# A two-layer diffusion step on one core: states and weights requested a step earlier, one gating result kept in SBUF, weight sums split in place

## The chip, the cores and the metric

The kernel runs on 1 core of one Trainium2 chip. The metric is device time in microseconds (us): the time that one launch takes on the core. Beside the times there is one profiled execution, whose trace records the instructions of each engine: PE (matmuls), DVE, ACT and POOL (elementwise work), and SP, whose queue issues the transfers.

## What is computed

A context of 128 tokens and 2048 latent tokens (2176 rows of 1024 numbers, float32) pass two layers, each with an RMS norm with scale and shift, an input projection, a mixer, an output projection and a gated residual. Layer 0, the one that the change touches, cut to what matters:

```python
q, k, v, ga, lr_f, lr_b, u, vs, gb = split_cols(h @ w_in_even, EVEN_SPLITS)
o_f, s_f = gla_scan(q, k, v, log_decay(lr_f, 0), s0_f)             # forward over the tokens
o_r, s_b = gla_scan(flip(q), flip(k), flip(v), flip(...), s0_b)    # backward
o_a = rmsnorm(o_f + flip(o_r), gla_norm_g) * silu(ga)              # branch A, 512 wide
sp  = einsum('hij,bnjhd->bnihd', w_s, rmsnorm(vs)) + b_s           # chunks of 128 tokens
o_b = u * sp * silu(gb)                                            # branch B, 512 wide
x   = x + gate * (concatenate([o_a, o_b]) @ w_out[0])
```

In `gla_scan` a state S of 64 x 128 for each head goes from one chunk of tokens to the next: `S = exp(b_last) * S + k'^T v`. Layer 1 has a pooling branch and a convolution branch; its input projection uses sums and differences of blocks of its weight matrix.

## The kernel before

A float32 product is made of three matmuls: every operand is kept as a rounded part *hi* (written by ACT) and the rest *lo* (DVE, or POOL for every third), both 128 x 512 for most tiles. `split` (L220) does that.

Layer 0 runs in four blocks of tokens (`block1`, L774; starts at about 0, 224, 415 and 612 us of the trace). A block makes its normed input `ring_hh`/`ring_hl` from `ring_xk` (`make_h`, L400), multiplies it with 20 groups of weight columns (`pg_g` is the PSUM tile of these products, two buffers), and has elementwise work evict each product. Weights come in through `load_w` (L229): raw from HBM and split in the first block that uses them, stored as hi and lo (`dr_w8h`, `dr_w8l`, for instance), and loaded from there in the later blocks (L235). Beside that, for every tile of 128 tokens, `gla_tile` computes the attention and the tile's contribution to the states: decays `Z` and `dec`, the contribution `ub` of the backward scan with its decay in a last column (L626, L627, L671), stored by L673 to `dr_ub`; the forward state `Sf` is stored by L664 to `dr_sf`.

Three pieces of work are put into this order a step at a time, one step after so many column groups (`tick`, L156; `side`, L183). A step ends at a `yield`.

- `prep_x` (L435) makes the next block's input: loads, squares summed on POOL, the norm, and then eight multiplications `make_t` on DVE (L391, 128 x 512). It begins after the first of the four gate groups.
- `weight_sums` (L743) makes 12 sets of sums for layer 1. A set loads two raw tiles of 128 x 1024 (L748), runs four POOL instructions (L760 to L768), stores one result to `dr_s` (L761), and splits three others (`part`): *hi* into a tile `px` (L753, ACT), *lo* over the sum itself (L755, DVE), and both stored to `dr_hl` (L757). The tag `px` has two buffers and is also used for the squares (L310). Two steps run at every third tick from the second block on; five steps are a set.
- The output projection of layer 0 (from about 869 us) runs over five blocks `BLKO`, the last tokens first, since the backward state goes from the last tile to the first. `finish_o` (L940) takes for each tile the state `Sb` from `states` (L922): two loads (L920, from `dr_sf` and `dr_ub`), then four DVE instructions (L934) that add the state of the tile after it, times its decay. Branch B's results lie in `dr_ob` (stored by L882, loaded back by `ob_part`). The first block `BLKO[0]` (tokens 1664 to 2176) is the last block of `block1`, and part of its work is done there.

A scheduler sets each engine's order when the kernel is built; an engine runs its instructions strictly in that order. All transfers are issued by SP from a single queue, also in order: where the next one waits for its data or its buffer, those behind it wait too. From about 1116 us on, layer 1 runs (four blocks of 544 tokens) to the end of the span.

## Time and profile before

| | us |
|---|---|
| median of 3 runs (lowest to highest) | 1888.07 (1882.71 to 1893.24) |
| the profiled execution | 1888.73 |
| its span in the trace | 1886.6 |
| PE busy | 1748.2 |
| DVE busy | 1196.5 |
| ACT busy | 845.5 |
| POOL busy | 741.6 |

The span is what the trace records from the first to the last instruction; the profiled execution takes 2.1 us more. In the views, `out<-in` names the tiles that an instruction writes and reads, and x4 is a count. PEclk is the clock that TensorE was granted, as a share of full speed; its two levels are 1.2 and 2.4 GHz. "Idle before" is the time that an engine sat idle ahead of an instruction, with the instruction or transfer that ended it; for a transfer, `a<-b` says that b was copied to a.

### The profile page before, as it was taken

The page shows a single profiled execution, that of the slowest core. Times are in us where ns is not written, and L with a number is a line of the kernel's source. Part 1 is how long each engine was busy: PE and PEld are TensorE (multiplying, and loading weights), DVE is VectorE, ACT ScalarE, POOL GpSimd, SP SyncE. Part 2 cuts the span into 40 slices and gives each one's busy share as a digit, 9 for nine tenths or more (in the row PEclk, how much of TensorE's full clock was granted, in tenths as well). Part 3 has the DMA queues.
Part 4 walks back from the last instruction along what each step waited for, and adds up shares of the span by engine and source line. Part 5 has one row for each costly group of instructions (what it writes and reads, how often), then busy time and mean ns, then how long its engine had stood idle before and what let it go on. Part 6 is the DMA issues. An engine that isn't in the chain of part 4 may idle for free. (4 is left out here: it accounts for less than half of the span.)

```text
span 1886.6 us, 39851 instructions
## 1 busy us (share of the span) xinstructions
PE 1748.2 (93%) x15115; PEld 1602.1 (85%) x15115; DVE 1196.5 (63%) x2270; ACT 845.5 (45%) x1795; POOL 741.6 (39%) x796
## 2 busy tenths in 40 slices
PE   5999899989999998999898999989999999999996
PEld 4877778768777897997687899989999999999996
DVE  5557852780679428656867775785758375837653
ACT  4544543451446326524534554554545354524431
POOL 0432543430453223335555562364335333532322
PEclk9999899999999998999898999999999999999998
DMA  9767787775766464476776478777977697659753
GB/s 327 270 227 252 283 301 251 250 252 209 279 224 227 147 242 149 148 231 180 235 243 213 140 264 263 248 254 260 320 241 227 208 326 241 217 189 329 233 185 130
DMA packets 232606, 444.15 MB, mean 235 GB/s; under 512 B 26208, under 2 KB 72032, under 8 KB 232416
## 3 DMA queue, kind: packets, MB, share of 16 engines
q1 hardware_dynamic: 232416, 441.62, 69.7%
q8 instruction: 119, 1.95, 0.4%
q14 instruction: 71, 0.58, 0.1%
HBM read 344.64 MB, written 96.88 MB: 234 GB/s over the span
## 5 line engine op out<-in xcount | busy, mean ns | idle before, releaser
L252 PE MATMUL pg_g<-t_t,wh_hi 128*128 128x272 f32 (+1 forms) x1920 | 371.0, 291 | 5.9 <-DVE tmp_ev L1328 3.0
L252 PEld LDWEIGHTS pg_g<-t_t,wh_hi 128*128 128x128 f32 x1920 | 302.1, 189 | 7.4 <-DVE tmp_ev L1328 3.6
L252 PE MATMUL pg_g<-t_t,wh_lo 128*128 128x280 f32 (+1 forms) x960 | 273.2, 290 | 2.0 <-DVE wh_lo L222 1.7
L252 PE MATMUL pg_g<-ring_hh,wp_hi 128*128 128x512 f32 (+2 forms) x632 | 234.8, 372 | 11.3 <-DVE tmp_ev L875 10.2
L252 PE MATMUL pg_g<-ring_hh,wp_lo 128*128 128x512 f32 (+2 forms) x632 | 230.4, 365 | 2.2 <-POOL wp_lo L222 1.9
L252 PE MATMUL pg_g<-ring_hl,wp_hi 128*128 128x512 f32 (+2 forms) x632 | 230.3, 364 | 0.0
L221 ACT ACTIVATE wh_hi<-wh_raw 128x512 fp32r<-128x512 f32 x208 | 130.6, 629 | 198.3 <-PE pg_g L252 137.7
L252 PEld LDWEIGHTS pg_g<-t_t,wh_lo 128*128 128x128 f32 x960 | 179.8, 189 | 2.8 <-DVE wh_lo L222 2.1
L252 PE MATMUL pg_g<-wp_hi,ring_hh 128*128 128x256 f32 (+1 forms) x528 | 161.0, 306 | 11.8 <-DMA wp_hi<-dr_w8h 3.3
L311 POOL TENSOR_TENSOR tmp_acc<-tmp_acc,tmp_px 128x512 f32<-128x512 f32 (+5 forms) x83 | 112.4, 1354 | 135.8 <-ACT tmp_px L310 132.2
L222 DVE TENSOR_TENSOR wh_lo<-wh_raw,wh_hi 128x512 fp32r<-128x512 f32 x156 | 125.8, 808 | 53.5 <-ACT wh_hi L221 44.6
L252 PE MATMUL pg_g<-wp_hi,ring_hl 128*128 128x256 f32 (+1 forms) x528 | 156.4, 298 | 3.4 <-DVE ring_hl L407 3.2
L252 PE MATMUL pg_g<-wp_lo,ring_hh 128*128 128x256 f32 (+1 forms) x528 | 156.6, 297 | 0.5 <-DMA wp_lo<-dr_w6l 0.5
L252 PE MATMUL px_x<-t_t,wh_hi 128*128 128x272 f32 (+1 forms) x768 | 151.3, 291 | 0.3 <-DVE tmp_ev L1277 0.3
L252 PEld LDWEIGHTS pg_g<-ring_hh,wp_hi 128*128 128x128 f32 x632 | 120.8, 191 | 31.6 <-DVE tmp_ev L875 10.7
L252 PE MATMUL pg_g<-o_oh,wh_hi 128*128 128x272 f32 (+2 forms) x448 | 130.4, 293 | 8.5 <-ACT o_oh L221 5.3
L252 PEld LDWEIGHTS pg_g<-ring_hh,wp_lo 128*128 128x128 f32 x632 | 121.0, 191 | 19.2 <-POOL wp_lo L222 2.1
L252 PEld LDWEIGHTS pg_g<-ring_hl,wp_hi 128*128 128x128 f32 x632 | 121.0, 191 | 14.8 <-issue 1.1
L252 PE MATMUL pg_g<-o_ol,wh_hi 128*128 128x272 f32 (+2 forms) x448 | 131.7, 295 | 1.3 <-DVE o_ol L222 1.3
L252 PE MATMUL pg_g<-o_oh,wh_lo 128*128 128x272 f32 (+2 forms) x448 | 131.3, 294 | 0.0
L566 POOL TENSOR_TENSOR gl_Z<-gl_Z 128x128 f32<-128x128 f32 x170 | 82.3, 504 | 124.6 <-DVE gl_Z L566 84.9
L550 ACT ACTIVATE gl_L<-gl_Z 128x256 f32<-128x256 f32 x204 | 83.2, 419 | 97.3 <-DVE gl_Z L566 75.5
(298 smaller groups left out, 4403.4 us busy)
## 6 DMA issues: line engine op xcount, KB each, us to landing
wh_raw<-in_w_dram SPq DMA_DIRECT2D x144, 256.0 KB, 3.6
wh_hi<-dr_hl SPq DMA_DIRECT2D x144, 256.0 KB, 3.5
wh_lo<-dr_hl SPq DMA_DIRECT2D x144, 256.0 KB, 3.9
wp_raw<-in_w_ada_dram SPq DMA_DIRECT2D x32, 512.0 KB, 5.1
wp_raw<-in_w_dram SPq DMA_DIRECT2D x24, 512.0 KB, 5.6
wh_raw<-dr_s SPq DMA_DIRECT2D x48, 256.0 KB, 3.8
wh_hi<-dr_wo SPq DMA_DIRECT2D x48, 256.0 KB, 4.5
wh_lo<-dr_wo SPq DMA_DIRECT2D x48, 256.0 KB, 4.8
```

Of the source, the lines that this page charges most:

```text
L221: act(out=hi, in_=src, func=AF.Copy)
L222: (eng or lo_engine()).tensor_tensor(out=lo, in0=src, in1=hi.bitcast(F32), op=ALU.subtract)
L252: mm(out=out, lhsT=a, rhs=b, start=start and i == 0, stop=stop and i == n - 1, skip_group_check=resumed)
L311: eng.tensor_tensor(out=acc, in0=acc, in1=sq, op=ALU.add)
L550: act(out=dst.rearrange("p (b t s) -> p t b s", t=2, s=s), in_=diag_ap(Z, 2 * i, s), func=AF.Exp, scale=1.0 / 16.0)
L566: (dve if i >= 2 or s < 4 else gps).tensor_tensor(out=dst, in0=dst, in1=bc(src), op=ALU.add)
```

## The change

- `prep_x` of the next block begins before the `vs` products (`gemm_tok(2 + u)`), not after the first gate group, and three steps lie between the norm and the first `make_t`.
- `dec` holds both decay columns; `ub` is taken only when its product `up` is done, and its column is copied from `dec`. That is one more DVE copy of 128 x 2 for 15 tiles.
- `weight_sums` has two empty steps between the loads and the first POOL instruction, and `part` writes *hi* over a sum that is no longer wanted (`A22`, then `A22` again, then `A21`) instead of into a `px` tile. A set is six steps, one at every tick.
- In the last block, branch B's result for the tokens of `BLKO[0]` is split from its tile `tmp_ev` into the operand tiles of the output projection. Four stores of 128 x 512 to `dr_ob` and four loads from it are gone.
- `state_in` issues the loads of the state for tile t-1 when `states(t)` has finished; `Sb` has three buffers in both pools.

Matmuls, ACT's and POOL's instructions keep their number. Line numbers shift: L391, L627, L753, L755, L757 and L875 of before are L390, L627/L628/L673, L757, L758, L760 and L879 of the changed kernel.

```diff
--- before.py
+++ after.py
...
@@ -450,7 +449,8 @@
             rr.append(r)
-        yield 1
+        for _ in range(3 if bi else 1):
+            yield 1
         for k in range(KT):
@@ -621,10 +623,9 @@
         if t:
-            dec = gl.tile([P, 2], F32, tag="dec", bufs=2)
-            dve.tensor_copy(out=dec, in_=Zv[:, 1, :, P - 1])
-            ub = gl.tile([P, 2, P + 1], F32, tag="ub", bufs=1)
-            dve.tensor_copy(out=ub[:, :, P], in_=Zv[:, 0, :, 0])
+            dec = gl.tile([P, 2, 2], F32, tag="dec", bufs=2)
+            dve.tensor_copy(out=dec[:, 0], in_=Zv[:, 1, :, P - 1])
+            dve.tensor_copy(out=dec[:, 1], in_=Zv[:, 0, :, 0])
         KE = Zv[:, 2:4]
@@ -664,10 +665,12 @@
             for pr in range(2):
-                dve.scalar_tensor_tensor(out=S[:, pr, :], in0=Sf[0][:, pr, :], scalar=dec[:, pr:pr + 1],
+                dve.scalar_tensor_tensor(out=S[:, pr, :], in0=Sf[0][:, pr, :], scalar=dec[:, 0, pr:pr + 1],
                                          in1=up[:, pr * P:(pr + 1) * P], op0=ALU.mult, op1=ALU.add)
...
             if t > 1:
+                ub = gl.tile([P, 2, P + 1], F32, tag="ub", bufs=1)
+                dve.tensor_copy(out=ub[:, :, P], in_=dec[:, 1])
                 act(out=ub[:, :, 0:P], in_=up[:, 256:512].rearrange("p (a b) -> p a b", a=2),
@@ -748,27 +751,28 @@
-            def part(j, s_):
-                hi = tmp.tile([P, width[0]], F32R, tag="px", bufs=width[4])[:, 0:512]
+            def part(j, s_, free):
+                hi, lo = (z.bitcast(F32R) for z in (free, s_))
                 act(out=hi, in_=s_, func=AF.Copy)
-                lo = s_.bitcast(F32R)
                 dve.tensor_tensor(out=lo, in0=s_, in1=hi.bitcast(F32), op=ALU.subtract)
...
+            yield 1
+            yield 1
...
             load(out=d_s[i], in_=A22)
-            yield 1
             gps.tensor_tensor(out=A21, in0=A11, in1=A21, op=ALU.subtract)
...
             gps.tensor_tensor(out=A11, in0=A22, in1=A11, op=ALU.subtract)
-            part(1, A21)
+            part(1, A21, A22)
             yield 1
             gps.tensor_tensor(out=A12, in0=A12, in1=A11, op=ALU.subtract)
-            part(0, A11)
             yield 1
-            part(2, A12)
+            part(0, A11, A22)
+            part(2, A12, A21)
             yield 1
@@ -778,7 +782,7 @@
         if bi == 1:
-            side(sums_, 3, 1, 2)
+            side(sums_, 1)
         v = [gl.tile([P, 512], F32, tag="v", bufs=6) for _ in range(nt)]
@@ -825,6 +829,9 @@
             glaq.append([0, gla_tile(TILES[bi][i], qk[i], v[i], lrT[i]), 0])
+        if bi + 1 < NB:
+            preps[bi + 1] = prep_x(bi + 1)
+            side(preps[bi + 1], 1)
@@ -865,9 +872,6 @@
                 load(out=d_g[bi][:, a // P:b // P, hh, :], in_=x.rearrange("p (i c) -> p i c", c=P))
-            if hh == PREP and bi + 1 < NB:
-                preps[bi + 1] = prep_x(bi + 1)
-                side(preps[bi + 1], 1)
         finish(mixer)
@@ -879,17 +883,24 @@
             for c0, t0, w in cols(bi):
-                load(out=d_ob[hh][:, t0:t0 + w], in_=t1_[:, c0:c0 + w])
+                if t0 == BLKO[0][0]:
+                    own_ob.append(t1_[:, c0:c0 + w])
+                else:
+                    load(out=d_ob[hh][:, t0:t0 + w], in_=t1_[:, c0:c0 + w])
             if hh == LATE and bi + 1 == NB:
...
                 open_late()
+            if opools:
+                for x in own_ob:
+                    ob0.append(o_tile(512, 0))
+                    split(x, *ob0[-1])
+                own_ob.clear()
...
     f2 = None
-    opools = []
     Sb = [None, None]
@@ -919,22 +930,34 @@
+    ahead = {}
+    def state_in(u):
+        own = fb[2] and u > BLKO[0][0] // P
+        S = (f2 if own else opools[0]).tile([P, 4, P + 1], F32, tag="Sb", bufs=3)
+        load_heads(S[0:64, :, 0:P], d_sf[u])
+        if u == NTILE - 1:
+            load_heads(S[64:P, :, 0:P], state[1])
+        else:
+            load_heads(S[64:P], d_ub[u + 1])
+        ahead[u] = S
     def states(t):
...
             u = NTILE - 1 if Sb[1] is None else Sb[1] - 1
-            own = fb[2] and u > BLKO[0][0] // P
-            S = (f2 if own else opools[0]).tile([P, 4, P + 1], F32, tag="Sb", bufs=fb[3] if own else 2)
-            load_heads(S[0:64, :, 0:P], d_sf[u])
-            if u == NTILE - 1:
-                load_heads(S[64:P, :, 0:P], state[1])
-            else:
-                load_heads(S[64:P], d_ub[u + 1])
+            if u not in ahead:
+                state_in(u)
+            S = ahead.pop(u)
+            if u < NTILE - 1:
                 for h in range(4):
...
             Sb[0], Sb[1] = S, u
+        if t > 1 and t - 1 not in ahead:
+            state_in(t - 1)
         return Sb[0]
@@ -949,8 +972,7 @@
                 hi, lo = o_tile(n, bi % 2)
-                x = (xx.tile([P, WOP], F32, tag="x", bufs=2) if bi else
-                     tmp.tile([P, 640], F32, tag="px", bufs=2))[:, 0:n]
+                x = xx.tile([P, WOP], F32, tag="x", bufs=2)[:, 0:n]
                 load(out=x, in_=d_ob[hh][:, t0:t1])
@@ -1004,7 +1026,7 @@
             yield None
-            ob_part()
+            o8.extend(ob0)
         yield o8
...
     def fin_o(bi, every, per=1, first=1):
```

The scheduler moves instructions with it, at these places among others.

DVE at the end of the second block, before. `ring_xk` is the next block's input; L875 evicts a product `pg_g` of the main chain of matmuls; `gl_ub` and `gl_Z` are the backward contribution and the decays of a tile:

```order
L627 COPY gl_ub_4749<-gl_Z_4232 128x2
L302 SCALAR_TENSOR_TENSOR tmp_r_4446<-tmp_nw_4583,tmp_nw_4585 128x512
L633 TENSOR_TENSOR gl_Z_4232<-gl_qk_2757,gl_Z_4232 128x512
L391 SCALAR_TENSOR_TENSOR ring_xk_3937<-ring_xk_3937,cst_gs_105,tmp_r_4446 128x512
L391 SCALAR_TENSOR_TENSOR ring_xk_3940<-ring_xk_3940,cst_gs_105,tmp_r_4446 128x512
L391 SCALAR_TENSOR_TENSOR ring_xk_4081<-ring_xk_4081,cst_gs_105,tmp_r_4446 128x512
L391 SCALAR_TENSOR_TENSOR ring_xk_4086<-ring_xk_4086,cst_gs_105,tmp_r_4446 128x512
L391 SCALAR_TENSOR_TENSOR ring_xk_4169<-ring_xk_4169,cst_gs_105,tmp_r_4446 128x512
L391 SCALAR_TENSOR_TENSOR ring_xk_4174<-ring_xk_4174,cst_gs_105,tmp_r_4446 128x512
L391 SCALAR_TENSOR_TENSOR ring_xk_4262<-ring_xk_4262,cst_gs_105,tmp_r_4446 128x512
L391 SCALAR_TENSOR_TENSOR ring_xk_4267<-ring_xk_4267,cst_gs_105,tmp_r_4446 128x512
L875 TENSOR_TENSOR tmp_ev_4593<-pg_g_4598,sg_vs_3306 128x512
```

And after, about forty rows earlier in the engine's order:

```order
L301 SCALAR_TENSOR_TENSOR tmp_r_3965<-tmp_nw_4112,tmp_nw_4114 128x512
L324 SCALAR_TENSOR_TENSOR tmp_ev_4159<-tmp_ev_4159,cst_glag_539,tmp_ev_4161 128x512
L390 SCALAR_TENSOR_TENSOR ring_xk_3400<-ring_xk_3400,cst_gs_105,tmp_r_3965 128x512
L390 SCALAR_TENSOR_TENSOR ring_xk_3403<-ring_xk_3403,cst_gs_105,tmp_r_3965 128x512
L390 SCALAR_TENSOR_TENSOR ring_xk_3491<-ring_xk_3491,cst_gs_105,tmp_r_3965 128x512
L390 SCALAR_TENSOR_TENSOR ring_xk_3496<-ring_xk_3496,cst_gs_105,tmp_r_3965 128x512
L390 SCALAR_TENSOR_TENSOR ring_xk_3580<-ring_xk_3580,cst_gs_105,tmp_r_3965 128x512
L390 SCALAR_TENSOR_TENSOR ring_xk_3585<-ring_xk_3585,cst_gs_105,tmp_r_3965 128x512
L390 SCALAR_TENSOR_TENSOR ring_xk_3752<-ring_xk_3752,cst_gs_105,tmp_r_3965 128x512
L390 SCALAR_TENSOR_TENSOR ring_xk_3757<-ring_xk_3757,cst_gs_105,tmp_r_3965 128x512
L361 COPY tmp_ev_4192<-ps_s_3296 128x256
L864 SCALAR_TENSOR_TENSOR sg_vs_3303<-ps_s_4121,cst_sgug_541,sg_bsb_545 128x128 x4
```

The copy into `gl_ub` is no longer ahead of the eight multiplications, and what stands behind them is an eviction of a norm product and of the `vs` mixer, not of `pg_g`.

SP's queue in the fourth block, before, from the raw loads of the ninth set of sums on. `dr_w8` and `dr_w9` are the weights of the next column groups:

```order
L748 DMA wp_raw_9191<-in_w_dram 128x1024
L748 DMA wp_raw_9192<-in_w_dram 128x1024
L761 DMA dr_s_95_561<-wp_raw_9192 128x512
L757 DMA dr_hl_107_573<-tmp_px_9764 128x512
L757 DMA dr_hl_107_573<-wp_raw_9192 128x512
L757 DMA dr_hl_107_573<-tmp_px_9770 128x512
L238 DMA wp_raw_10587<-in_wo_dram 128x1024
L757 DMA dr_hl_107_573<-wp_raw_9191 128x512
L235 DMA wp_lo_8423<-dr_w8l_1190 128x1024
L235 DMA wp_hi_8422<-dr_w8h_1189 128x1024
L235 DMA wp_lo_8923<-dr_w9l_1425 128x1024
L235 DMA wp_hi_8922<-dr_w9h_1424 128x1024
```

And after, from the raw loads of the eleventh set on:

```order
L751 DMA wp_raw_9222<-in_w_dram 128x1024
L751 DMA wp_raw_9223<-in_w_dram 128x1024
L234 DMA wp_lo_8441<-dr_w8l_1209 128x1024
L234 DMA wp_hi_8440<-dr_w8h_1208 128x1024
L234 DMA wp_lo_8953<-dr_w9l_1464 128x1024
L234 DMA wp_hi_8952<-dr_w9h_1463 128x1024
L766 DMA dr_s_97_563<-wp_raw_9223 128x512
L636 DMA dr_qe_31_136<-gl_Z_8113 128x2x256
L760 DMA dr_hl_109_575<-wp_raw_9223 128x512 x2
```

Before, the loads of the two weights stand behind the store to `dr_s` and the four stores to `dr_hl` of the set that was loaded ahead of them; now they stand right behind the raw loads, ahead of all of these.

ACT near the end of the third block, before, around the three copies (L753) of the seventh set of sums; the other rows belong to a tile's attention:

```order
L753 ACTIVATE tmp_px_7469<-wp_raw_7029 128x512
L533 ACTIVATE gl_Z_6477<-pm_m_6472 128x512
L534 ACTIVATE gl_Z_6477<-gl_Z_6477 128x512
L753 ACTIVATE tmp_px_7475<-wp_raw_7028 128x512
L535 ACTIVATE gl_Z_6477<-gl_Z_6477 128x512
L550 ACTIVATE gl_Q_198_6483<-gl_Z_6477 128x2x128
L753 ACTIVATE tmp_px_7722<-wp_raw_7028 128x512
```

And after, the eighth set, which has come to this place (L757):

```order
L757 ACTIVATE wp_raw_6733<-wp_raw_6733 128x512
L535 ACTIVATE gl_Z_6534<-pm_m_6529 128x512
L536 ACTIVATE gl_Z_6534<-gl_Z_6534 128x512
L537 ACTIVATE gl_Z_6534<-gl_Z_6534 128x512
L757 ACTIVATE wp_raw_6733<-wp_raw_6732 128x512 x2
L552 ACTIVATE gl_Q_197_6540<-gl_Z_6534 128x2x128
L616 ACTIVATE gl_A_6005<-pm_m_6596 128x2x2x128
```

The second copy writes the tile that the first wrote (`wp_raw_6733`), three rows behind it, and the third follows at once.

## Rows read from the trace of the kernel before

**Rows 1.** The page, part 1: busy time, share of the span, instructions of each engine
```profile
PE 1748.2 (93%) x15115; PEld 1602.1 (85%) x15115; DVE 1196.5 (63%) x2270; ACT 845.5 (45%) x1795; POOL 741.6 (39%) x796
```

**Rows 2.** Busy time by stretch: eight stretches of layer 0, then all of layer 1
```profile
core 0: us, PE busy (x) PEld busy (x) DVE busy (x) ACT busy (x) POOL busy (x), PEclk, DMA share, GB/s
205.00:255.00 50.00, 40.29 (x407) 35.09 (x406) 42.97 (x85) 26.69 (x53) 25.85 (x30) 0.83 0.72 244
390.00:430.00 40.00, 31.24 (x386) 26.49 (x385) 32.43 (x67) 17.30 (x35) 12.75 (x19) 0.87 0.66 219
525.00:575.00 50.00, 42.98 (x406) 34.78 (x405) 39.00 (x76) 22.16 (x46) 24.69 (x26) 0.93 0.69 235
593.00:630.00 37.00, 30.87 (x363) 25.79 (x363) 32.78 (x72) 19.25 (x40) 12.62 (x18) 0.91 0.34 124
685.00:760.00 75.00, 67.03 (x1166) 61.11 (x1167) 49.37 (x128) 36.33 (x93) 25.58 (x36) 0.89 0.50 175
805.00:870.00 65.00, 58.56 (x374) 55.59 (x373) 39.55 (x66) 26.52 (x59) 27.88 (x27) 0.97 0.65 198
880.00:940.00 60.00, 50.91 (x211) 39.67 (x210) 48.77 (x64) 29.90 (x58) 32.42 (x27) 0.91 0.75 229
990.00:1060.00 70.00, 57.61 (x289) 54.40 (x288) 49.72 (x67) 32.89 (x66) 41.22 (x36) 0.88 0.64 201
1116.00:1868.00 752.00, 731.50 (x5637) 724.55 (x5636) 476.88 (x866) 339.25 (x682) 295.27 (x302) 0.99 0.74 246
```

**Rows 3.** Waits of PE in 0 to 1116: total us, times, longest
```profile
PE pg_g L252 <- DVE tmp_ev L875: 10.2, 3, 5.4
...
PE ps_s L284 <- ACT tmp_px L221: 9.8, 4, 4.1
...
PE ps_s L649 <- DVE gl_A L618: 7.9, 3, 3.7
...
PE pg_g L252 <- DMA wp_hi<-dr_w8h: 3.3, 1, 3.3
```

**Rows 4.** Timeline of DVE, 390 to 398: start, duration, [idle before <-releaser]
```profile
390.32 0.17 DVE L627 COPY gl_ub<-gl_Z 128x2 f32<-128x2 f32 x1 [2.44 <-DMA dr_ub<-gl_ub]
...
391.60 5.38 DVE L391 SCALAR_TENSOR_TENSOR ring_xk<-ring_xk,cst_gs,tmp_r 128x512 f32<-128x512 f32 x8
...
396.90 0.68 DVE L875 TENSOR_TENSOR tmp_ev<-pg_g,sg_vs 128x512 f32<-128x512 f32 x1
```

**Rows 5.** Timeline of DVE in the first output projection, 990 to 1026
```profile
994.67 1.75 DVE L755 TENSOR_TENSOR wp_raw<-wp_raw,tmp_px 128x512 fp32r<-128x512 f32 x1
...
1017.81 3.62 DVE L934 SCALAR_TENSOR_TENSOR oA_Sb<-oA_Sb,oA_Sb 64x128 f32<-64x128 f32 x4 [1.97 <-DMA oA_Sb<-dr_ub]
```

**Rows 6.** Waits of DVE and ACT for transfers, 0 to 1116
```profile
DVE oA_Sb L934 <- DMA oA_Sb<-dr_ub: 19.5, 9, 3.7
...
DVE gl_ub L627 <- DMA dr_ub<-gl_ub: 12.1, 6, 6.4
...
ACT oA_oh L221 <- DMA tmp_px<-dr_ob: 16.6, 4, 7.1
...
ACT tmp_px L753 <- DMA dr_hl<-tmp_px: 9.9, 5, 3.2
```

**Rows 7.** By line, ns min/median/max: weight sums, their stores' landing, then L934
```profile
L753 ACT ACTIVATE tmp_px<-wp_raw x36: 614/630/653, 234.0 to 1038.9; 128x512 fp32r<-128x512 f32 x36
...
L760 POOL TENSOR_TENSOR wp_raw<-wp_raw x12: 1280/1289/1927, 227.8 to 1015.7; 128x512 f32<-128x512 f32 x12
...
DMA to landing us min/median/max: 2.0/4.0/9.1
...
L934 DVE SCALAR_TENSOR_TENSOR oA_Sb<-oA_Sb,oA_Sb x48: 347/356/1494, 844.0 to 1034.2; 64x128 f32<-64x128 f32 x48
```

**Rows 8.** Timeline of SP's queue, 688 to 701: start, us, DMA issued
```profile
688.88 2.29 SPq L748 DMA_DIRECT2D wp_raw<-in_w_dram  x2
700.30 0.33 SPq L761 DMA_DIRECT2D dr_s<-wp_raw  x1
```

More of the change, by code (lines that the diff above doesn't have):

```diff
@@ L48 @@
 STAG = 6
-PREP = 0
 RATE = 2
@@ L460 @@
     preps = {}
+    own_ob, ob0 = [], []
+    opools = []
     s0 = ExitStack()
```

## The prediction

> **What bounds the kernel now.** First I read the page's busy times: PE works 1748.2 of 1886.6 us [rows 1], so PE sets the time, and only what makes PE wait, or makes it work at the lower clock, can be won back. Then the busy time by stretch says where that is. Layer 1, which the change does not touch, is 731.5 of 752 us busy at a granted clock of 0.99; there is nothing in it for this change. In the eight stretches of layer 0 PE is idle for 9.7, 8.8, 7.0, 6.1, 8.0, 6.4, 9.1 and 12.4 us (the length less PE's busy time), together 67.5 of 447 us [rows 2]. There the clock is also granted at 0.83 to 0.97: length times what lacks to 1 is 44.5 us, and since PE works for 0.85 of these stretches, about 38 us of its work are lost so. Idle time and low clock lie in the same stretches, while layer 1, with little idle time, has almost the full clock. So I count every us of idle time that goes as 1 + 38/67.5 = 1.56 us. That ratio is an average that I choose; a stall of 3 us can cost nothing more, or the same again.
>
> Next the waits of PE: 10.2 us in three for L875, 9.8 in four for the squares of the norm in the output projection, 7.9 in three for L618, and 3.3 in one for a weight [rows 3]. These 31.2 us are what the edits aim at. The other waits are many, of 0.3 to 3 us, behind a DVE that is 86% busy in 205 to 255 and 89% in 593 to 630 [rows 2]; they are work that comes late, not an engine that stands.
>
> **Norm input earlier, and the copy for the backward state.** The timeline of DVE shows the longest wait: at 390.32 the copy into `gl_ub` had waited 2.44 us for the store of the tile before, then eight multiplications of 5.38 us together ran, and only then, at 396.90, the eviction that PE was waiting for [rows 4]. In the new order the copy is gone from there and no `pg_g` eviction stands behind the eight: 5.4 us [rows 3]. The copy's longest wait, 6.4 us [rows 6], lies in 525 to 575, where PE then waits 3.7 us for L618 [rows 3]: 3.7. Of the other 4.2 us for L618 I take half, 2.1, since its DVE queue has the norm's work ahead in the second block. In 593 to 630, where the eight of the fourth block stood just ahead of the block's own `ring_hl`, I take 2.0 of 6.1 us [rows 2]. The price is 15 more copies of 0.17 us [rows 4], 2.6 us of DVE; I cost it at nothing, because it lies beside matmuls while DVE still has room (81% busy at 390 to 430 [rows 2]), and at 2.6 if that cover is gone. Sum: 13.2 us of idle time.
>
> **Weights behind the sums' stores.** SP issued two raw loads at 688.88 and nothing more until 700.30, when the first of the sums was ready to be stored [rows 8]; the weights behind it came late, 3.3 us of PE [rows 3]. Two empty steps and the new order put them ahead: 3.3. The same can come up for the two weights that now stand behind the tenth set's store; they are loaded several column groups ahead, so I count nothing for it, and 3.3 as its bound.
>
> **States a step ahead.** DVE waits 19.5 us in nine for `oA_Sb` [rows 6]. What of it reaches PE is read at 1017.81: a wait of 1.97, then four instructions of 3.62 us that take 4 x 0.36 = 1.4 when alone [rows 5, 7], 4.2 us together, about as much as the longest wait of PE for the squares, 4.1 [rows 3]. I take 4.1. Another 1.75 comes from the sums: L755 stood in front of the next norm at 994.67 [rows 5], and three of the twelve sets were made in the output projection, one is now. Sum: 5.9.
>
> **Branch B from SBUF.** Four stores and four loads go, and ACT's 16.6 us of waiting for them [rows 6]. ACT is not late for PE in most of that time: of the 10.2 us for L875, 4.8 lie in 805 to 870, and I take half, 2.4; and 2.0 of the 9.1 us in 880 to 940 [rows 2], where the last of the loads fell. The splits themselves stay.
>
> So 13.2 + 3.3 + 5.9 + 4.4 = 26.8 us of idle time, by 1.56: 41.8 us.
>
> **Sums in place: what it costs.** A *hi* written over a sum has to wait until that tile's store has landed. Before, it waited for one of two `px` tiles, five times, 9.9 us or 2.0 each [rows 6]. Now two of a set's three copies write a tile that the same set has just stored, 24 in all, and in the order on ACT they stand three to nine rows apart, in about half of the sets three to five; a store lands after 2.0 to 9.1 us, in the median 4.0 [rows 7]. The nearest row is the old wait of 2.0, and I take it for all 24: 48 us of ACT, from 0 to 24 x 4.0 = 96 by the bounds. How much of it reaches PE? The waits of DVE for transfers, 19.5 + 12.1 = 31.6 us [rows 6], cost PE 2.4 + 3.7 + 2.0 = 8.1 by the steps above, a quarter. A quarter of 48 is 12, by 1.56: 18.7 us. The two sets that move into the four blocks bring 4 x 1.29 on POOL, 3 x 0.63 on ACT [rows 7] and 3 x 0.68 on DVE (the eviction of that size [rows 4]), 9.1 us each, 18.2 in all on engines that mostly have room; I take a tenth, 1.8, with 0 and 18.2 as bounds.
>
> The Trainium skill speaks against this part in two places. The page "DMA: Bandwidth & Descriptors", section "Anatomy of one DMA — SWDGE (gpsimd) path", puts a fixed cost of about 2.0 us on a transfer, most of it the receipt from the target memory, longest for HBM. The fastest store here took 2.0 us and the median 4.0 [rows 7]; with the page's figure alone the wait of 2.0 would about vanish, and the sum, an estimate, would be 1848. The page "GPSIMD Engine Reference", section "1. Specifications", says that POOL shares its SBUF interfaces with VectorE, which contends in instructions with two SBUF inputs. L934 is one, and it goes from 0.35 to 1.49 us [rows 7]; no run here has shown POOL to be the cause. If the POOL work of the two sets, 10.3 us, reached PE in full, the time would be 1881.
>
> **Sum.** 41.8 - 18.7 - 1.8 = 21.3 us. From the profiled execution's 1888.73 that gives 1867.4; it lies 0.66 above the median of the runs, so 1867.
>
> **Rivals.** *All of it, without new waits.* The stores land before ACT comes back (the empty steps put the copies later), and the four rows of waits go whole with 4 us of the rest: 35.2 x 1.56 = 54.9 us, 1833. For it: ACT is only 45% busy [rows 1], so it is early rather than late; against it: the three to five rows.
>
> *The waits go, and the work behind them is late instead.* DVE is at 86 to 89% in the stretches of the block changes [rows 2], so when its stalls go, the eight multiplications only hold up another eviction. Then the waits that are pure transfer remain as gain, 3.7 + 3.3 + 5.9 = 12.9 us, by 1.56 20.1; the cost of 20.5 stays: 1888, no change.
>
> *Slower: ACT stops for its own stores.* One mechanism: the second and third copy of each set wait on ACT in order, and behind them stand the `gl_Z` and `gl_A` copies that PE's next matmuls need, and DVE's *lo*, behind which evictions of `pg_g` stand. If three quarters of the 48 us reach PE, it costs 36 x 1.56 = 56.2 and 1.8 against 41.8: 1904. It decides from 25.6 of the 48 us on, 53%, where it eats the whole gain.
>
> **How the numbers follow.** The forecast, 1846 to 1878, has 0.50; all of it 0.14; no change 0.21; slower 0.15. The range reaches from 1836 to 1896: it leaves out about 0.06 below (a part of the first rival) and 0.13 above. A difference under 0.5%, 9.4 us, is about what a measurement of this kernel cannot tell from none; so faster (under 1878.6) 0.65, same 0.20, slower (over 1897.5) 0.15.
>
> **What would show it.** Right: no wait of DVE for `dr_ub` at the copy into `gl_ub`, PE's 5.4 us for L875 gone, no stop of SP ahead of `dr_w8`, hardly any wait at the state's instructions, granted clock up in the first seven stretches. Wrong: waits of ACT for `dr_hl` of much over 48 us in all, or DVE's *lo* held up by ACT, with PE late right behind; or a layer 1 that changes by more than 2 us, which nothing here explains; or low clock that stays while the idle time goes, which would leave 26.8 - 12 - 1.8 = 13.0 us of gain.

## The result, and the profile after

The changed kernel takes 1876.46 us in the median of 7 runs (1869.75 to 1878.41), against 1888.07 before: a ratio of 0.9929, with a 95% interval of 0.9908 to 0.995. It is 11.6 us faster. The prediction was 1867 with a range of 1836 to 1896, so the time lies in the range and on the forecast side, with about half of the forecast gain of 21. The profiled execution of the changed kernel took 1872.58 us; the parts below are read against 1888.73 of before.

The busy times of the changed kernel's page, which answer to [rows 1]:

```profile
PE 1732.2 (93%) x15115; PEld 1587.0 (85%) x15115; DVE 1182.9 (63%) x2285; ACT 840.9 (45%) x1795; POOL 742.4 (40%) x796
```

PE is busy 16.0 us less for the same 15115 instructions, and the span is 15.8 us shorter. Where that lies is best read by stage. The next two fences are the busy times in stretches that begin at the first `pg_g` matmul of each block (the fourth at 607.5 us before); the first fence is of before, with the four input blocks and the output projection:

```profile
core 0: us, PE busy (x) PEld busy (x) DVE busy (x) ACT busy (x) POOL busy (x), PEclk, DMA share, GB/s
0.00:223.60 223.60, 188.80 (x1913) 151.61 (x1913) 140.63 (x266) 107.95 (x209) 68.92 (x79) 0.98 0.77 272
223.60:414.90 191.30, 180.83 (x1921) 151.94 (x1915) 118.77 (x259) 83.92 (x193) 76.36 (x94) 0.95 0.75 263
414.90:607.50 192.60, 178.53 (x1763) 148.13 (x1757) 114.20 (x244) 81.42 (x188) 68.93 (x80) 0.97 0.70 241
607.50:868.90 261.40, 240.87 (x2792) 223.76 (x2791) 155.12 (x372) 111.23 (x271) 79.98 (x112) 0.95 0.53 177
868.90:1115.60 246.70, 223.99 (x1093) 199.46 (x1092) 179.85 (x252) 118.67 (x248) 146.48 (x126) 0.94 0.69 216
```

And of the changed kernel, the last row being layer 1:

```profile
0.00:217.90 217.90, 189.68 (x1992) 154.34 (x1992) 139.62 (x280) 106.05 (x212) 72.63 (x86) 0.96 0.79 276
217.90:418.50 200.60, 182.77 (x1844) 151.32 (x1834) 126.54 (x261) 86.21 (x196) 78.22 (x91) 0.95 0.78 268
418.50:621.00 202.50, 179.79 (x1850) 149.83 (x1838) 120.38 (x267) 85.37 (x198) 73.61 (x88) 0.95 0.72 244
621.00:865.60 244.60, 231.90 (x2715) 214.44 (x2711) 144.84 (x357) 106.72 (x264) 80.37 (x107) 0.99 0.56 187
865.60:1098.80 233.20, 214.29 (x1093) 191.90 (x1092) 160.88 (x240) 113.07 (x238) 133.54 (x116) 0.96 0.62 194
1098.80:1853.60 754.80, 731.82 (x5649) 724.14 (x5648) 479.99 (x867) 340.39 (x685) 298.83 (x304) 0.99 0.74 246
```

Three things can be read here. First, layer 1 stayed as it was (before, it lasted 753.8 us between the same matmuls).

Second, the output projection became shorter, 246.7 to 233.2, and the fourth block too, 261.4 to 244.6, while the second and third block became longer, 191.3 to 200.6 and 192.6 to 202.5. But the stretches do not hold the same work. The counts behind PE show it (1921 to 1844 in the second, 2792 to 2715 in the fourth): 80 small matmuls of a tile's attention, with the elementwise work around them, have moved out of the second block into the first, and 80 out of the fourth into the third. So the blocks are to be read in pairs: first and second together went from 414.9 to 418.5, third and fourth from 454.0 to 447.1. Of the 16.8 us that layer 0 gained, 13.5 lie in the output projection.

Third, the idle time of PE (length less busy time) has hardly changed in sum: 34.8 + 10.5 + 14.1 + 20.5 + 22.7 = 102.6 us before, 28.2 + 17.8 + 22.7 + 12.7 + 18.9 = 100.3 after. What fell is PE's busy time, 1013.0 to 998.4 us. The granted clock rose from 0.95 to 0.99 in the fourth block and from 0.94 to 0.96 in the output projection, and fell from 0.98 to 0.96 in the first and from 0.97 to 0.95 in the third; the last section says how that goes with the busy time.

A stage of a single trace is good to a few us: the first block lasted 217.9 to 224.8 us in the traces of kernels that differ from the changed one only in the sums, which do not run there.

The waits of PE in layer 0 of the changed kernel (total us, times, longest), against [rows 3]:

```profile
...
PE ps_s L283 <- ACT tmp_px L220: 8.6, 3, 6.9
...
PE ps_s L861 <- POOL gl_Z L540: 7.3, 1, 7.3
...
PE pm_m L586 <- DVE gl_L L557: 6.7, 3, 4.6
...
PE ps_s L650 <- DVE gl_A L620: 6.0, 4, 3.4
...
PE pg_g L251 <- DVE tmp_ev L879: 3.4, 2, 2.0
...
PE pg_g L251 <- DMA wp_hi<-dr_w8h: 1.4, 1, 1.4
```

Of the four waits that the edits aimed at, three are shorter: 10.2 to 3.4 for the eviction (L879 now), 7.9 to 6.0 for `gl_A`, 3.3 to 1.4 for `dr_w8`. The fourth, for the squares in the output projection (L283 now), is nearly as long, 9.8 to 8.6, and its longest went from 4.1 to 6.9. New ones stand beside them, one of 7.3 us for the `vs` mixer (L861) and 6.7 for the levels of the attention (L586). The waits of DVE and ACT for transfers, against [rows 6]:

```profile
DVE oA_Sb L955 <- DMA oA_Sb<-dr_ub: 8.6, 6, 3.0
...
DVE gl_ub L673 <- DMA dr_ub<-gl_ub: 5.8, 3, 4.2
...
ACT wp_raw L757 <- DMA dr_hl<-wp_raw: 9.9, 8, 2.8
...
ACT wp_raw L757 <- DMA dr_s<-wp_raw: 2.8, 2, 1.8
```

The states' wait fell from 19.5 to 8.6 and that of the backward contribution from 12.1 to 5.8; the prediction had expected the latter to be gone. The two ACT rows are the new waits for stores before a rounded part may be written in place: 12.7 us in ten, where the prediction counted 48 in 24. (All three copies of a set write over a tile that the set has stored, since the first goes over the sum that went to `dr_s`; so there are 36 such places, not 24.)

The longest new wait, followed back: POOL, ACT, DVE and PE near 550 to 564 us, at the end of the third block:

```profile
548.95 1.29 POOL L765 TENSOR_TENSOR wp_raw<-wp_raw 128x512 f32<-128x512 f32 x1 [14.84 <-DMA wp_raw<-in_w_dram]
```

```profile
552.98 0.63 ACT L757 ACTIVATE wp_raw<-wp_raw 128x512 fp32r<-128x512 f32 x1 [6.52 <-POOL wp_raw L769]
```

```profile
553.65 1.22 DVE L758 TENSOR_TENSOR wp_raw<-wp_raw 128x512 fp32r<-128x512 f32 x1 [5.55 <-DMA dr_g<-tmp_ev]
554.79 7.21 DVE L390 SCALAR_TENSOR_TENSOR ring_xk<-ring_xk,cst_gs,tmp_r 128x512 f32<-128x512 f32 x15
561.93 0.68 DVE L538 SCALAR_TENSOR_TENSOR gl_Z<-pm_m,gl_Z 128x512 f32<-128x512 f32 x1
```

```profile
563.93 0.77 PE L861 MATMUL ps_s<-sg_wst,sg_vs 128*128 128x128 f32 x2 [7.29 <-POOL gl_Z L540]
```

The raw tile of a set of sums lands, POOL begins at 548.95, ACT's rounded part comes at 552.98, and DVE, which stands at the remainder L758 for 5.55 us (put down to a store, but ACT's part had ended just then), has 15 multiplications of 7.21 us behind it and only then, at 561.93, the L538 that the attention goes on from. PE waits 7.29 us. At the end of the second block, where [rows 4] had a wait for a store ahead of the multiplications, PE's 5.4 us are gone; here, one block later, a wait for the sums stands ahead of such multiplications.

### The profile page after: what moved, and what is told of

It is laid out like the page before. It is cut to its first block, busy times and chain, and to the rows that moved or that the text cites. A ratio compares the mean times of both kernels' runs of the same rounds, so it can differ in the third digit from the quotient of the medians.

```text
span 1870.8 us, 39817 instructions
## 1 busy us (share of the span) xinstructions
PE 1732.2 (93%) x15115; PEld 1587.0 (85%) x15115; DVE 1182.9 (63%) x2285; ACT 840.9 (45%) x1795; POOL 742.4 (40%) x796
## 4 chain that ended last, share of the span: by engine, by line
PE 54%; DVE 15%; DMA 9%; issue 3%; ACT 3%; POOL 2%; SPq 0%; DVEq 0%; POOLq 0%; ACTq 0%
PE pg_g L251 43%; PE px_x L251 7%; DVE gl_Z L568 2%; DMA dr_hl<-wp_raw 2%; DMA e_xk<-dr_x 1%; DMA wp_raw<-in_w_dram 1%; DVE e_xk L390 1%; DVE t_t L221 1%; DVE gl_L L557 1%; DVE gl_A L620 1%; PE ps_s L356 1%; DVE wp_raw L758 1%; DMA wh_hi<-dr_hl 1%; PE ps_s L1403 1%; POOL gl_Z L568 1%
## 5 line engine op out<-in xcount | busy, mean ns | idle before, releaser
L251 PE MATMUL pg_g<-t_t,wh_hi 128*128 128x272 f32 (+1 forms) x1920 | 370.8, 291 | 7.6 <-ACT tu_U L1476 4.3
L251 PEld LDWEIGHTS pg_g<-t_t,wh_hi 128*128 128x128 f32 x1920 | 301.7, 189 | 9.3 <-ACT tu_U L1476 4.6
L251 PE MATMUL pg_g<-t_t,wh_lo 128*128 128x280 f32 (+1 forms) x960 | 272.9, 290 | 1.9 <-DVE wh_lo L221 1.5
L251 PE MATMUL pg_g<-ring_hh,wp_hi 128*128 128x512 f32 (+2 forms) x632 | 236.0, 373 | 5.7 <-DVE tmp_ev L879 3.4
L251 PE MATMUL pg_g<-ring_hh,wp_lo 128*128 128x512 f32 (+2 forms) x632 | 231.3, 366 | 1.6 <-POOL wp_lo L221 1.0
L251 PE MATMUL pg_g<-ring_hl,wp_hi 128*128 128x512 f32 (+2 forms) x632 | 230.4, 365 | 0.0
L251 PEld LDWEIGHTS pg_g<-t_t,wh_lo 128*128 128x128 f32 x960 | 179.5, 189 | 2.7 <-DVE wh_lo L221 1.9
L251 PE MATMUL pg_g<-wp_hi,ring_hh 128*128 128x256 f32 (+1 forms) x528 | 157.3, 298 | 9.6 <-ACT gl_v L798 5.0
L251 PE MATMUL pg_g<-wp_hi,ring_hl 128*128 128x256 f32 (+1 forms) x528 | 152.8, 291 | 1.8 <-DVE ring_hl L406 1.7
L251 PE MATMUL pg_g<-wp_lo,ring_hh 128*128 128x256 f32 (+1 forms) x528 | 152.4, 289 | 1.1 <-DMA wp_lo<-dr_w6l 0.6
L251 PE MATMUL px_x<-t_t,wh_hi 128*128 128x272 f32 (+1 forms) x768 | 151.4, 291 | 1.6 <-DVE tu_s L1299 1.3
L251 PEld LDWEIGHTS pg_g<-ring_hh,wp_hi 128*128 128x128 f32 x632 | 121.5, 192 | 26.8 <-DVE tmp_ev L879 4.0
L568 POOL TENSOR_TENSOR gl_Z<-gl_Z 128x128 f32<-128x128 f32 x170 | 89.6, 545 | 128.8 <-DVE gl_Z L568 93.0
L251 PEld LDWEIGHTS pg_g<-ring_hh,wp_lo 128*128 128x128 f32 x632 | 121.3, 192 | 19.2 <-POOL wp_lo L221 1.1
L251 PE MATMUL pg_g<-o_oh,wh_hi 128*128 128x272 f32 (+2 forms) x448 | 130.2, 293 | 7.3 <-ACT o_oh L220 5.1
L251 PEld LDWEIGHTS pg_g<-ring_hl,wp_hi 128*128 128x128 f32 x632 | 121.6, 192 | 15.7 <-issue 1.3
L251 PE MATMUL pg_g<-o_ol,wh_hi 128*128 128x272 f32 (+2 forms) x448 | 130.6, 292 | 2.0 <-DVE o_ol L221 2.0
L251 PE MATMUL pg_g<-o_oh,wh_lo 128*128 128x272 f32 (+2 forms) x448 | 130.5, 292 | 1.1 <-DMA wh_lo<-dr_wo 1.1
```

What stands on the lines that cost most here:

```text
L251: mm(out=out, lhsT=a, rhs=b, start=start and i == 0, stop=stop and i == n - 1, skip_group_check=resumed)
L568: (dve if i >= 2 or s < 4 else gps).tensor_tensor(out=dst, in0=dst, in1=bc(src), op=ALU.add)
```

## The experiments

The table has the ratio to the runs of before on the same chip with its interval, and from one trace each the length of a stage as above, in us. In u1 the matmuls lie in the blocks as they do before, in all other variants as in the changed kernel.

| kernel | ratio | first | second | third | fourth block | output |
|---|---|---|---|---|---|---|
| before | 1 | 223.6 | 191.3 | 192.6 | 261.4 | 246.7 |
| changed | 0.9929 (0.9908 to 0.995) | 217.9 | 200.6 | 202.4 | 244.6 | 233.2 |
| u1 | 0.9977 (0.9957 to 0.9998) | 220.6 | 205.6 | 193.5 | 252.6 | 230.1 |
| u2 | 0.9961 (0.9947 to 0.9974) | 223.1 | 203.5 | 198.4 | 247.6 | 233.3 |
| u3 | 0.9900 (0.9874 to 0.9926) | 219.8 | 193.2 | 191.1 | 245.2 | 240.5 |
| u4 | 0.9937 (0.9918 to 0.9955) | 221.3 | 201.1 | 203.0 | 244.7 | 228.0 |
| u5 | 0.9972 (0.9957 to 0.9987) | 221.8 | 200.7 | 200.6 | 250.7 | 232.5 |
| v1 | 0.9944 (0.9922 to 0.9966) | 220.6 | 200.6 | 196.2 | 248.0 | 231.9 |
| v2 | 0.9900 (0.9880 to 0.9919) | 221.9 | 195.4 | 194.7 | 248.5 | 238.6 |
| w1 | 0.9925 (0.9905 to 0.9945) | 223.3 | 192.5 | 194.2 | 248.9 | 246.0 |
| w2 | 0.9928 (0.9909 to 0.9947) | 224.7 | 198.3 | 192.2 | 246.5 | 239.7 |
| w3 | 0.9909 (0.9890 to 0.9928) | 224.8 | 191.1 | 195.5 | 245.3 | 243.7 |
| w4 | 0.9868 (0.9846 to 0.9889) | 222.1 | 192.5 | 195.4 | 250.6 | 228.4 |
| w5 | 0.9867 (0.9850 to 0.9883) | 219.9 | 195.2 | 191.8 | 259.6 | 221.5 |

### Each part undone (u1 to u5)

u1 puts the start of the next norm input back:

```diff
-        if bi + 1 < NB:                      # ahead of the vs products
-            preps[bi + 1] = prep_x(bi + 1)
-            side(preps[bi + 1], 1)
+            if hh == 0 and bi + 1 < NB:      # behind the first gate group
+                preps[bi + 1] = prep_x(bi + 1)
+                side(preps[bi + 1], 1)
-        for _ in range(3 if bi else 1):
-            yield 1
+        yield 1
```

> The changed kernel with one part undone: the next block's norm input starts after the first gate group again, with one step before its multiplications. The changed kernel stands at 0.993 of before. Between 225 and 638 us its trace has lost 8 us against before, with PE waiting 7.29 us at 563.93 behind 15 multiplications of 7.21 us on DVE. Theory S (the sums at one step per tick eat the gain of these blocks): nothing or a loss here, ratio 0.993 to 0.997, and 225 to 638 stays within 3 us. Rival M (the multiplications, now in front of the attention's L538, eat it): 4 to 8 us faster, ratio 0.989 to 0.991, all of it in 225 to 638.

It is slower, 0.9977: neither expectation. The earlier input is worth 0.48%, some 9 us, and the intervals lie apart. At the end of the second block the old picture is back, multiplications on DVE right ahead of the eviction (L878 here), and PE waiting for it:

```profile
404.78 4.06 DVE L390 SCALAR_TENSOR_TENSOR ring_xk<-ring_xk,cst_gs,tmp_r 128x512 f32<-128x512 f32 x6
408.75 0.68 DVE L878 TENSOR_TENSOR tmp_ev<-pg_g,sg_vs 128x512 f32<-128x512 f32 x1
```

```profile
409.49 0.80 PE L251 MATMUL pg_g<-ring_hh,wp_hi 128*128 128x512 f32 x1 [5.57 <-DVE tmp_ev L878]
```

The second block is 5 us longer. The third falls by 9, as rival M wanted, and the fourth rises by 8, but there the 80 attention matmuls have moved back as well; the two together last 446.1 us in u1 and 447.0 in the changed kernel. So the lengths show neither a gain in the fourth block nor a price in the third. The trace of u1 is of an execution of 1876.72 us, 6 below the median of its runs, and holds only a part of the loss.

u2 takes the buffer of the backward contribution early again:

```diff
-            dve.tensor_copy(out=dec[:, 1], in_=Zv[:, 0, :, 0])
+            ub = gl.tile([P, 2, P + 1], F32, tag="ub", bufs=1)
+            dve.tensor_copy(out=ub[:, :, P], in_=Zv[:, 0, :, 0])
```

> The changed kernel with one part undone: the buffer of the backward contribution is taken before its product again, with the copy of the decay in front of the state's other work. DVE waits 12.1 us for its stores in before and 5.8 in the changed kernel. If these waits reach PE as the prediction had it (5.4 and 3.7 us of idle time, times 1.56): 5 to 12 us slower, ratio 0.996 to 0.999. If they are hidden behind other late work: within 3 us, 0.992 to 0.994.

0.9961, in the range of the first case: the part is worth 0.32%, about 6 us, though the two intervals still overlap a little. In which stage, one trace does not tell. The wait that the edit was made for does not explain it. DVE's wait for the stores of `ub`, in u2 and then in u1, which has the late buffer:

```profile
DVE gl_ub L629 <- DMA dr_ub<-gl_ub: 7.6, 3, 3.8
```

```profile
DVE gl_ub L672 <- DMA dr_ub<-gl_ub: 16.1, 4, 7.6
```

Without the late buffer the wait is 1.8 us longer than the changed kernel's 5.8; with the late buffer, but with the norm input at its old place, it is longer than before the change (12.1).

u3 puts the old sums back, code and pace:

```diff
-            side(sums_, 1)
+            side(sums_, 3, 1, 2)
-                hi, lo = (z.bitcast(F32R) for z in (free, s_))
+                hi = tmp.tile([P, width[0]], F32R, tag="px", bufs=width[4])[:, 0:512]
...
-            yield 1
-            yield 1
```

> The changed kernel with one part undone: the weight sums write their rounded parts into px tiles again, with no empty steps, two steps at every third tick. Theory S (sums eat the gain of blocks 2 to 4): 225 to 638 us becomes 6 to 10 us shorter than in the changed kernel, and the output projection, which gets three sets back, 5 to 9 us longer: ratio 0.989 to 0.994. Rival M: 225 to 638 stays within 3 us, and the output projection alone is longer: ratio 0.996 to 0.999.

This is theory S in its direction and its ratio: the second and third block are 18.7 us shorter together, about twice what it said, the output projection is 7.3 longer, and the ratio 0.9900 is better than with the change, though the intervals overlap.

u4 loads the states when they are needed:

```diff
-            if u not in ahead:
-                state_in(u)
-            S = ahead.pop(u)
+            S = (f2 if own else opools[0]).tile([P, 4, P + 1], F32, tag="Sb", bufs=fb[3] if own else 2)
+            load_heads(S[0:64, :, 0:P], d_sf[u])
...
-        if t > 1 and t - 1 not in ahead:
-            state_in(t - 1)
```

> The changed kernel with one part undone: the states are loaded when they are needed, with two and three buffers. The changed kernel gains 13.4 us in the output projection (861 to 1093 us of its trace). If that comes from the states' loads: 6 to 12 us slower, ratio 0.996 to 0.999, with DVE waiting near 19 us for them again. If it comes from the sums that left the output projection: 0 to 3 us slower, 0.993 to 0.995.

DVE waits for the states again:

```profile
DVE oA_Sb L945 <- DMA oA_Sb<-dr_ub: 17.0, 9, 3.7
```

17.0 us where the changed kernel waits 8.6, and the time is the same within the intervals, 0.9937, which is the second case. So in this kernel the wait costs nothing that can be measured.

u5 sends branch B through DRAM:

```diff
-                if t0 == BLKO[0][0]:
-                    own_ob.append(t1_[:, c0:c0 + w])
-                else:
-                    load(out=d_ob[hh][:, t0:t0 + w], in_=t1_[:, c0:c0 + w])
+                load(out=d_ob[hh][:, t0:t0 + w], in_=t1_[:, c0:c0 + w])
...
-            o8.extend(ob0)
+            ob_part()
```

> The changed kernel with one part undone: branch B's result of the first output block is stored and loaded back. The last input block became 16.8 us shorter by the change (261.4 to 244.6), of which 8 came back when the norm input was put back. If the way through DRAM is what cost there: 244.6 becomes 250 to 254 and the output projection 1 to 4 us longer, ratio 0.996 to 1.000. If it was hidden: within 3 us, ratio 0.992 to 0.994.

The part is worth 0.43%, about 8 us, with intervals that lie apart, and it lies where it was expected: the fourth block is 6.1 us longer. The output projection is not longer (232.5 against 233.2), where 1 to 4 us had been expected. The longest wait of PE for an eviction in the fourth block, in the changed kernel and in u5:

```profile
PE pg_g L251 <- DVE tmp_ev L879: 2.0, 1, 2.0
```

```profile
PE pg_g L251 <- DVE tmp_ev L879: 6.4, 1, 6.4
```

### In place, or the pace (v1, v2)

v1 keeps the new pace and writes into `px` tiles; v2 keeps the old pace and writes in place:

```diff
-                hi, lo = (z.bitcast(F32R) for z in (free, s_))     # v1
+                hi = tmp.tile([P, width[0]], F32R, tag="px", bufs=width[4])[:, 0:512]
+                lo = s_.bitcast(F32R)
...
-            side(sums_, 1)                                         # v2, and old yields
+            side(sums_, 3, 1, 2)
```

> The changed kernel, whose weight sums keep the new pace (a step at every tick, two empty steps) but write the rounded parts into px tiles instead of in place. With the old sums the second and third block took 193.2 and 191.1 us, with the new ones 200.6 and 202.4. Theory P (the pace: one more set in each of these blocks, its steps at every tick ahead of the attention's work): both blocks stay near 200 and 202 us, ratio 0.992 to 0.995. Rival I (writing in place: ACT waits for the stores, DVE behind it): both blocks fall to 191 to 194 us and the output projection stays at 233, ratio 0.985 to 0.989.

> The changed kernel with the weight sums at the old pace (two steps at every third tick, no empty steps), but with the rounded parts written in place. Theory P: second and third block at 191 to 195 us as with the old sums, output projection near 240, ratio 0.989 to 0.991. Rival I: the blocks stay at 198 us or more, and the output projection too is longer than 240, ratio 0.995 or above.

Both ratios come out as theory P has it; of the blocks, v2's second is 0.4 us outside its range, and v1's third, 196.2, lies between the two theories. At the new pace the second and third block are long (396.8 together) without a part in place, and at the old pace they are shorter (390.1) with them. v1 and u3, both with `px` tiles, differ only in the pace and the order of the steps: 0.9944 and 0.9900, with intervals that just touch. v2 is as fast as u3, 0.9900, though its ACT waits for stores:

```profile
ACT wp_raw L756 <- DMA dr_hl<-wp_raw: 11.6, 12, 2.5
...
ACT wp_raw L756 <- DMA dr_s<-wp_raw: 4.6, 2, 2.8
```

16.2 us of such waits, and nothing of it in the time. (In single traces the second and third block together are some 6 us longer in place at either pace, 403.0 against 396.8 and 390.1 against 384.3; the ratios do not show it.)

### States ahead, with the old sums (w1)

The edits of u3 and u4 together.

> The changed kernel with the sums as before and the states loaded when needed: the norm input, the late buffer and branch B remain. The old sums alone gave 0.990; loading the states late alone 0.9937, with an output projection of 228.0 against 233.2 us in one trace each. If the states ahead are worth nothing also with the old sums: 0.988 to 0.991. If they pay where sums run in the output projection too (22 us of idle PE there): 4 to 8 us slower than with the old sums alone, 0.992 to 0.995.

0.9925 is in the second case's range and speaks for states that pay, against 0.9900 for u3, and the output projection takes 246.0 instead of 240.5 us. But the two intervals overlap, and DVE's waits do not bear it out. With the old sums and the states late (w1):

```profile
DVE oA_Sb L944 <- DMA oA_Sb<-dr_ub: 17.8, 9, 4.0
DVE f_Sb L944 <- DMA f_Sb<-dr_ub: 11.3, 2, 7.2
```

And with the old sums and the states ahead (u3):

```profile
DVE oA_Sb L954 <- DMA oA_Sb<-dr_ub: 29.7, 12, 5.4
...
DVE f_Sb L954 <- DMA f_Sb<-dr_ub: 4.2, 2, 2.4
```

(`f_Sb` are the states of the last tiles, which lie in another pool.) DVE waits 29.1 us in all in w1 and 33.9 in u3. With the old sums, issuing the loads a step ahead did not shorten the wait, and the kernel that waits more has the better ratio. That the states ahead are worth something with the old sums is not shown, and if they are, it is not by this wait.

### Where the sums go (w2 to w5)

w2 keeps the new order with longer sets; w3 is v2 with a slower pace; w4 and w5 are v2 with a fast fourth block. The sets that run in the second, third and fourth block and in the output projection are 4, 3, 2, 3 before and in u3, v2, w1 and w2; 5, 4, 2, 1 in the changed kernel; 3, 3, 1, 5 in w3; 4, 3, 3, 2 in w4; 4, 3, 5, 0 in w5.

```diff
-            yield 1
-            yield 1
+            for _ in range(3 + i % 2):             # w2
+                yield 1
...
-            side(sums_, 3, 1, 2)
+            side(sums_, 4, 1, 2)                   # w3
...
+        if bi + 1 == NB:
+            for e in later:
+                if e[2] is sums_:
+                    e[1] = e[3] = 1                # w4; w5: e[1], e[3] = 1, 2
```

> The changed kernel (in place, a step at every tick) with three or four empty steps in a set instead of two, so that the second and third block make about as many sets as before. Theory P1 (what costs there is the extra set's work on POOL, ACT and DVE): the two blocks fall from 200.6 and 202.4 to 192 to 197 us, the output projection rises to 237 to 241, ratio 0.989 to 0.991. Theory P2 (what costs is the order, a step of the sums in front of the attention at every tick): the blocks stay at 199 to 203 us and the output projection still rises, ratio 0.994 to 0.997.

The two blocks fell by 12.5 us, which speaks for the extra set (P1), but the ratio did not move: 6.5 went back to the output projection, and the first block, where no sums run, was 6.8 longer in this trace. P1 is supported by the stages, not shown by the time.

> The old pace made slower (two steps at every fourth tick instead of every third), in place, all else as in the changed kernel. Against the old pace (0.990; blocks 195.4 and 194.7, output projection 238.6). If each set costs the second and third block 5 us or more, as the comparison of the paces says, and the output projection about 3: the blocks 188 to 192 us, the output projection 241 to 245, ratio 0.987 to 0.989. If only the set too many costs, and a block takes three or four for nothing: the blocks within 2 us, ratio 0.991 to 0.994.

Between the two: the second block is at 191.1, the third at 195.5, the output projection at 243.7, and 0.9909 lies in neither range. Against v2, moving one set out of the second and one out of the fourth block into the output projection brings nothing.

> The old pace in the second and third block, one step at every tick in the fourth, in place. The fourth block has five tiles and PE idle for 12.7 of 244.6 us. If it takes one more set for nothing: 244 to 249 us there and an output projection of 235 to 237 (238.6 with the old pace), ratio 0.987 to 0.990. If a set costs there what it costs in the second and third: 251 to 255 us, ratio 0.990 to 0.993.

> As the kernel with one step at every tick in the fourth block (0.9868; fourth block 250.6, output projection 228.4 us), but two steps at every tick there, so that no set, or hardly one, is left for the output projection. If the fourth block takes sets more cheaply than the output projection: fourth block 251 to 255, output projection 221 to 226, ratio 0.983 to 0.987. If two sets more crowd the attention there as they did in the second and third block (5 us and more a set): fourth block above 258, ratio 0.988 to 0.992.

Both are faster than the changed kernel: its interval begins above the ends of theirs. The rows of w4, second block to output projection:

```profile
222.10:414.60 192.50, 180.60 (x1846) 149.14 (x1834) 123.99 (x258) 85.36 (x193) 72.85 (x87) 0.97 0.76 265
414.60:610.00 195.40, 179.66 (x1846) 149.85 (x1837) 114.25 (x261) 83.03 (x191) 69.99 (x84) 0.96 0.70 237
610.00:860.50 250.50, 235.29 (x2714) 217.26 (x2710) 151.62 (x363) 110.86 (x270) 80.06 (x111) 0.98 0.59 196
860.50:1088.90 228.40, 213.86 (x1092) 191.39 (x1092) 167.71 (x243) 114.07 (x242) 138.43 (x121) 0.98 0.68 211
```

Against v2 one set more runs in the fourth block, for 2 us there, and the output projection is 10.2 shorter. In w5 two more sets cost the fourth block 9.0 and save the output projection 6.9; so the block is crowded, as the second case had it (above 258), and the output projection and the ratio, 0.9867, are those of the first. w4 came out at the first case's ratio or just below it; its fourth block is a little over that case's 249, and its output projection is well below 235. w4 and w5, at 1865.29 and 1863.15 us in the median, beat both kernels.

## Why the prediction was right, and where it was not

The sign and the range were right; the gain came out at about half, with errors that partly cancel. That the time fell in the range is in part luck: the loss that was written large, for the copies in place, was not there, the gains were written twice too large, and a loss that was written small came.

**The factor of 1.56.** It is not borne out. The prediction took 26.8 us of idle time away, put 13.8 back, and counted clock in proportion. In sum idle time fell by 2.3 us and PE's busy time by 14.6. In the fourth block 7.8 us of idle time went with 9.0 of busy time; in the output projection 3.8 with 9.7; in the first 6.6 us of idle time went and 0.9 of busy time came; in the second and third 16 us of idle time came and only 3.2 of busy time. The doubt in the text ("a stall of 3 us can cost nothing more, or the same again") was nearer the truth than the average. The reading that the other waits of PE are 0.3 to 3 us long left out one of 13.9 us at the start of the first block (L298), which is there in both kernels.

**Norm input and backward contribution** (13.2 us of idle time, 20.6 with the factor). Undone one at a time they cost 9 and 6 us. The wait of 5.4 us for L875 is gone as predicted, and comes back with 5.57 us when the norm input is put back (u1): this step is shown. But the step "no `pg_g` eviction stands behind the eight" looked at one kind of victim only: the attention's L538 and the mixer stand behind them now, 7.29 us of PE in the third block. That is the rival "the work behind them is late instead", true in one place. That the late buffer removes DVE's wait for its stores is not borne out (u2, u1); how it is worth 6 us stays open.

**Branch B from SBUF** (4.4, 6.9 with the factor): 8 us by u5, at the place that was named. **States ahead** (4.1 of 5.9): nothing with the new sums by u4, and nothing that is clear of noise with the old ones by w1. The step that failed is from DVE's wait to PE: PE's wait for the squares, from which the 4.1 were taken, stayed (9.8 to 8.6). **Weights behind the stores**: 3.3 became 1.4; not isolated in time. One by one the parts cost 9, 6 and 8 us when undone, 23 together; less the 5 us that the pace costs (below) that would leave 18, where 11.6 were measured, so the parts do not simply add.

**Sums in place** (18.7 us of loss). This term was not there: 12.7 us of waits instead of 48, and no time for 16.2 of them in v2. The failing step is taking the old wait of 2.0 us for every place; in ten of 36 a store was still under way, for 1.3 us in the mean, and a quarter reaching PE was too much. With it falls the rival "slower", which needed 25.6 us of waiting at PE.

**The sets moved into the blocks** (1.8 us of loss, bound 18.2). This is the term that was too small. Putting the pace back is worth 0.29%, about 5 us: 0.9900 in both u3 and v2, against 0.9928 to 0.9944 in four kernels with the new order (changed, u4, v1, w2). Each of these four intervals overlaps with at least one of those two; it is the agreement that speaks for it. By stages, with the new pace the second and third block together take 397 to 404 us (changed kernel, u4, u5, v1), with the old one 384 to 390 (u3, v2, w1), some 14 us for two sets, of which the output projection gives 8 or so back. That the two sets are the cause is not shown: w2 has as many sets in each stage as v2 and as short a second and third block (390.5), and yet its ratio is that of the changed kernel. "Engines that mostly have room" was read from busy shares, 62% of the second block's time on DVE before; the chain through POOL, ACT and DVE that each set forms in front of the attention, as at 548.95 to 563.93 above, is not in a share.

The Trainium skill's page "GPSIMD Engine Reference", section "1. Specifications", says that POOL shares its SBUF interfaces with VectorE, with contention for DVE instructions in a 2-port mode or with two SBUF inputs. Whether that or the order of the queues makes the loss, no run here separates.

Without the new pace the rest of the change is worth 18.9 us (v2 and u3, 0.9900). So: gross gain about 19 where 41.8 was written, in-place cost none that the time shows where 18.7 was written, pace about 5 where 1.8 was written.

Still open: why w2 is no faster than the changed kernel, why the second and third block seem to lose more by one set each than the fourth does, and in which stage the late backward buffer pays.

## What to carry to other kernels

Before moving background work to where an engine is idle on average, look at what stands behind each of its steps in the engines' queues: here, by stages of single traces, one more set of sums cost two blocks about 7 us each, the fourth block 2 to 5, and the output projection 3 to 10. The length of a wait on a transfer does not say what it is worth: 8 us more of it for the states (u4) and 16.2 us of it for the stores (v2) cost nothing here. A change to the order of the work also moves work over the border of a stage, so compare the counts before the lengths. After moving a run of instructions off one victim, name the next instruction behind it.

## What the hardware showed that was not expected

The change left PE's idle time in layer 0 nearly as it was, and 14.6 of the 16.8 us came as less busy time for the same matmuls. The mean granted clock of layer 0 hardly tells it, 0.96 in both kernels, because it counts idle time too. The trace's clock records, laid over PE's busy time, do: PE was busy at the lower level for 81.9 us before and for 58.2 after. With half the work done in a us at that level this makes 11.9 of the 14.6 us (an estimate). The time at the lower level itself fell less, from 92.1 to 82.0 us: more of it now lies on idle time. What a stretch with two long waits costs is seen here in the changed kernel, from 925 to 950 us, where PE waited 4.4 and 6.9 us:

```profile
925.00:950.00 25.00, 14.21 (x43) 10.72 (x44) 20.74 (x29) 12.26 (x27) 15.87 (x13) 0.59 0.72 217
```

PE worked 14.21 of 25 us at a mean granted clock of 0.59; its two levels are 1.2 and 2.4 GHz, so most of that stretch ran at the lower one. The matmuls L251 show the two levels: from 943.43 us on, two start 0.42 us apart, from 947.10 on 0.23.

A store of the sums to `dr_hl` landed in 3.6 us in the median in the changed kernel and 4.0 in the one before, and 26 of 36 copies in place did not have to wait for theirs.
